# Narrow pooling bands, blocks of the first unit ended one by one, re-placed attention stages and a tail on four engines in a hybrid attention block

## The chip, the core and the metric

The kernel runs on one NeuronCore of a Trainium2 chip. The metric is the device time of one execution in microseconds. A kernel's time is the median of several executions; beside them one execution was profiled, and all rows of the profile come from that one. PE is TensorE, PEld its weight loads, DVE VectorE, ACT ScalarE, POOL GpSimd, SP the engine whose queue issues most DMAs.

## What is computed

One decoder layer for 1024 positions of width 1024, float32 throughout:

```python
h = rms_norm(x, ln_pre_mix)
proj = h @ w_in                       # 256 pooling channels, then q, k, v of 12 heads of 64
pool_out = multi_scale_pool(u_pool, w_pool, pool_scale)   # windows 2/4/8/16, 4 groups of 64 channels
attn_out = dilated_attention(rope(q), rope(k), v)          # windows (128,1), (512,4), (2048,16)
mix = concat(pool_out, attn_out) @ w_out
x = x + rms_norm(mix, ln_post_mix)
h = rms_norm(x, ln_pre_ffn)
f = (silu(h @ w_gate) * (h @ w_up)) @ w_down
x = x + rms_norm(f, ln_post_ffn)
```

In the pooling mixer each group's channels are averaged over a trailing window, the token itself is subtracted, and a 64x64 map and a per-channel scale follow.

## The kernel before

**Products.** Activations lie transposed, channels on the partitions. Each float32 operand is split into a high and a low part (`split`, `into`), ACT copying the high part and DVE or POOL subtracting for the low one; a product is then three matmuls (`PASSES`: high-high, high-low, low-high).

**Stages.** First the norm and the q/k projection of head pair 0. Then the "first unit" with `rows_first`, which projects the values of pairs 0 and 1 and the pooling channels together, in two halves of 512 positions; each half has four blocks of 128 positions, four weight tiles `i` and two contraction tiles `kk` in each, and one PSUM bank per block (`pj` for blocks 0 and 1, `t` for 2 and 3, two buffers each). When a block has its last product, ACT and DVE take it out as high and low parts, into the tile `vs` (one buffer, two blocks fill it, then one DMA stores it to `vd`) and into `u`. Then `pool_bands` and `pool_means` make the window means as products of `u` with a band matrix, 144 columns wide (a block and the 16 positions after it), and `pool_product` applies the 64x64 maps.

**Attention units.** Six head pairs times two halves are twelve units, numbered by `turn_of`. A unit has these stages: `scores` (8 steps; DVE masks and takes the maximum in one instruction, ACT exponentiates), `merge`/`join` (the weights `wv` from maxima and sums, small DVE steps around one pair of small matmuls `e`), `weigh` (16 scalings of score blocks by `wv`, on POOL or DVE), `turn` (PE transposes the weighted blocks, ACT and DVE split them into `ptr`) and `product` (values). `rope` of later pairs and the projections of later q, k and v run between them.

**What sets the order.** PE executes in program order. `put(steps, lo, hi)` places each stage's steps on a time axis whose unit is an attention unit; `emit` sorts all steps by place. The table `PRM` (`G`) holds the places: `h0`, `h1` for units of the first and second half, `first` and `last` for the end units, `du` for additions per unit, `pm` for the bands, `c0` to `c3` for norm chains and block sums after the attention. `Fill` lists hold projection matmuls; `await_` pulls further fill steps ahead of a stage while the planner's own clock is below the stage's due time, at most `fl` of them. On the other engines a scheduler orders the instructions, and `high_priority(offset)` ranks the small stages (score masks and exponentials, merges, the splits of `turn`) above their place; `hp` is that offset, doubled for a merge. `wd` says for each of the 16 scalings whether POOL (0) or DVE (1) takes it, `we` which `w_in` tiles are split by DVE (1) instead of POOL, `rk`, `rq`, `r0` to `r3` on which engine a rope's sine product and its sum run (0 POOL, 1 DVE).

**After attention.** `out_proj` in two halves, norms (`chain`), the gated feed-forward as seven block products per pair of tiles (`seven`), after six tiles' first products (`firsts`), then the down projection (`down`, products P1 to P3 in the order P1, P6, P2, P7, P4, P5, P3). The last product P3 is cut into columns 0 to 256 and 256 to 512, each ended by `End.finish`: `mean` (PE sums the squares of `sq` and of the last square `jk`), a POOL power, `rows` (PE transposes the factors into a PSUM row block `rb`), `times` (DVE multiplies four 128-row blocks at once) and `plus` (adds `x`, then stores).

Of the kernel before, what the change touches and what calls it, by code (L numbers as in the profile page):

```python
# [1765 lines left out]
```

## Time and profile before

| | |
|---|---|
| median of 3 runs | 1148.39 us |
| lowest, highest | 1147.02, 1149.25 us |
| profiled execution, its own time | 1147.94 us |
| its span, first to last instruction | 1146.2 us |
| PE busy | 1122.9 us (98%), 5916 matmuls |
| PE weight loads | 964.5 us (84%) |
| DVE, ACT, POOL busy | 825.2 (72%), 553.0 (48%), 548.6 us (48%) |
| DMA | 201.59 MB, 176 GB/s over the span |
| mean granted clock of PE | 0.989 |

Matmuls are pipelined, so PE's busy time says that something was in the array, not that it streamed at its peak; the ends of matmuls are modelled, and a few matmul records can be missing. A row of the timeline reads: start, length, engine, line, operation, output tile, inputs, shape, number of instructions merged, and in brackets how long the engine sat idle before it and which instruction ended that. A wait is put down to the semaphore that came last by the profile; where the engine named had long been done, it was another.

### The profile page before, as it was taken

Reading aid. Unit: us, or ns where it says so; the run is one execution under the profiler, and the core shown is the slowest. Engines: PE = TensorE matmul, PEld = TensorE weight load, DVE = VectorE, ACT = ScalarE, POOL = GpSimd, SP = SyncE. Lnnn points to the kernel's source line nnn. Section 1 sums busy time; section 2 is a strip of 40 time slices with the busy share of each in tenths; the row PEclk is TensorE's granted clock in tenths of the full one; section 3 lists DMA queues with packets and bytes.
Section 4 is the critical chain, followed back from the end, with each engine's and each line's share of the span. In section 5 each row is a group of like instructions: output and inputs, shape, how many; then the busy total and the mean of one; then the engine's idle time right before and its main releaser. Section 6 shows DMA issues by size and latency. Waiting matters only on the chain. (4 is left out here: it accounts for less than half of the span.)

```text
span 1146.2 us, 16886 instructions
## 1 busy us (share of the span) xinstructions
PE 1122.9 (98%) x5916; PEld 964.5 (84%) x5916; DVE 825.2 (72%) x1525; ACT 553.0 (48%) x1048; POOL 548.6 (48%) x488
## 2 busy tenths in 40 slices
PE   9999999999998999999999999999999999999996
PEld 7888998989888888888888888888888888888896
DVE  7956888887988684979867777675666477343684
ACT  7345766666666674767422222332233425343441
POOL 0030535364465222020067677875587859666520
PEclk9998999999998999999999999999999999999998
DMA  8215151515126655754566666433543879566442
GB/s 279 99 59 187 39 183 38 183 39 184 56 92 219 204 201 193 286 198 170 193 210 239 244 249 235 173 126 140 202 166 150 283 261 312 193 198 199 131 147 74
DMA packets 91140, 201.59 MB, mean 176 GB/s; under 512 B 9264, under 2 KB 25136, under 8 KB 89648
## 3 DMA queue, kind: packets, MB, share of 16 engines
q1 hardware_dynamic: 90080, 199.74, 50.0%
q8 instruction: 46, 0.75, 0.3%
q10 hardware_dynamic: 976, 0.79, 0.2%
q14 instruction: 38, 0.31, 0.1%
HBM read 143.61 MB, written 56.89 MB: 175 GB/s over the span
## 5 line engine op out<-in xcount | busy, mean ns | idle before, releaser
L167 PE MATMUL ps_o<-tT,fw 128*128 128x512 f32 x648 | 151.2, 390 | 0.0
L167 PEld LDWEIGHTS ps_o<-tT,fw 128*128 128x128 f32 x648 | 121.4, 188 | 26.2 <-issue 0.3
L167 PE MATMUL ps_pj<-x,whl 128*128 128x512 f32 x480 | 142.9, 411 | 0.0
L1249 POOL TENSOR_TENSOR fw<-rw,fw 128x512 fp32r<-128x512 f32 x74 | 103.2, 1418 | 29.5 <-ACT fw L1247 29.4
L702 POOL TENSOR_SCALAR pp<-pp,wv 128x256 f32<-128x256 f32 (+1 forms) x144 | 70.8, 511 | 71.3 <-DVE wv L682 71.3
L639 ACT ACTIVATE pp<-pp,sx 128x128 f32<-128x128 f32 (+1 forms) x192 | 89.2, 467 | 29.5 <-DVE sx L636 28.6
L213 POOL TENSOR_TENSOR whl<-wraw,whl 128x512 fp32r<-128x512 f32 x40 | 53.1, 1351 | 87.0 <-ACT whl L209 79.7
L167 PEld LDWEIGHTS ps_pj<-x,whl 128*128 128x128 f32 x480 | 85.8, 190 | 9.8
L1544 POOL TENSOR_TENSOR op<-rw,op 128x512 fp32r<-128x512 f32 x38 | 61.1, 1607 | 40.4 <-ACT op L1543 38.6
L239 POOL TENSOR_TENSOR nrr<-nrr,half 128x4 f32<-128x4 f32 (+1 forms) x7 | 7.4, 1060 | 142.7 <-ACT eps L238 99.4
L167 PE MATMUL ps_s<-b,fw 128*128 128x512 f32 x312 | 73.3, 392 | 0.0
L167 PE MATMUL ps_pj<-whl,x 128*128 128x256 f32 (+1 forms) x432 | 72.1, 305 | 0.3 <-POOL whl L213 0.3
L1545 DVE TENSOR_TENSOR op<-rw,op 128x512 fp32r<-128x512 f32 x33 | 45.2, 1369 | 34.4 <-ACT op L1543 34.3
L167 PEld LDWEIGHTS ps_s<-b,fw 128*128 128x128 f32 x312 | 58.6, 188 | 13.0
L1543 ACT ACTIVATE op<-rw 128x1024 fp32r<-128x1024 f32 x38 | 40.0, 1058 | 60.4 <-PE ps_t L167 30.3
L1249 POOL TENSOR_TENSOR whl<-rw,whl 128x512 fp32r<-128x512 f32 x30 | 47.4, 1602 | 42.2 <-ACT whl L1247 26.9
L1247 ACT ACTIVATE fw<-rw 128x1024 fp32r<-128x1024 f32 x45 | 47.5, 1061 | 40.5 <-PE ps_o L167 16.0
L747 ACT ACTIVATE ptr<-ps_t 128x512 fp32r<-128x512 f32 (+1 forms) x84 | 48.5, 577 | 37.0 <-PE ps_t L170 34.1
L748 DVE TENSOR_TENSOR ptr<-ps_t,ptr 128x512 fp32r<-128x512 f32 (+1 forms) x84 | 56.0, 667 | 13.7 <-ACT ptr L747 13.3
L167 PEld LDWEIGHTS ps_pj<-whl,x 128*128 128x128 f32 x432 | 60.1, 194 | 2.2 <-POOL whl L213 0.5
L167 PE MATMUL ps_o<-ptr,v 128*128 128x128 f32 (+1 forms) x472 | 57.4, 256 | 0.6 <-DVE ptr L748 0.6
L167 PEld LDWEIGHTS ps_o<-ptr,v 128*128 128x128 f32 x472 | 52.6, 164 | 3.9 <-DVE ptr L748 1.1
(312 smaller groups left out, 2862.6 us busy)
## 6 DMA issues: line engine op xcount, KB each, us to landing
rw<-bd SPq DMA_DIRECT2D x77, 256.0 KB, 4.1
rw<-in_w_gate_dram SPq DMA_DIRECT2D x28, 512.0 KB, 4.6
rw<-in_w_up_dram SPq DMA_DIRECT2D x28, 512.0 KB, 5.4
v<-vd SPq DMA_DIRECT2D x22, 512.0 KB, 3.9
rw<-wsd SPq DMA_DIRECT2D x44, 256.0 KB, 3.8
bd<-p SPq DMA_DIRECT2D x39, 256.0 KB, 2.2
rw<-in_w_down_dram SPq DMA_DIRECT2D x33, 256.0 KB, 3.9
wraw<-in_w_out_dram SPq DMA_DIRECT2D x15, 512.0 KB, 4.5
```

Source lines behind the costliest of these rows:

```text
L167: return tc.keep_in_program_order(nc.tensor.matmul(*a, **k))
L213: pin(eng.tensor_tensor(dst[:, 1, at:at + w], src[:, at:at + w], dst[:, 0, at:at + w].bitcast(F32), ALU.subtract))
L239: powers.append(nc.gpsimd.tensor_tensor(r, r, half.to_broadcast([P, n]), ALU.pow))
L639: nc.scalar.activation(pt[:, j, lo:], pt[:, j, lo:], AF.Exp, bias=sx[:, 0, side, j, hd, 0:1], scale=-1.0, accum_out=sx[:, 0, side, j, hd, ...
L702: nc.gpsimd.tensor_scalar(pv, pv, un.wv[:, side, j, hd:hd + 1], 1.0, op0=ALU.mult, op1=ALU.mult)
L747: nc.scalar.activation(ptr[:, 0, :w], t[:, :w], AF.Copy)
L748: nc.vector.tensor_tensor(ptr[:, 1, :w], t[:, :w], ptr[:, 0, :w].bitcast(F32), ALU.subtract)
L1247: nc.scalar.activation(dst[:, :, 0], src, AF.Copy)
L1249: low[0] = eng.tensor_tensor(dst[:, i, 1], src[:, i], dst[:, i, 0].bitcast(F32), ALU.subtract)
L1543: nc.scalar.activation(w[:, :, 0], raw, AF.Copy)
L1544: nc.gpsimd.tensor_tensor(w[:, 0, 1], raw[:, 0], w[:, 0, 0].bitcast(F32), ALU.subtract)
L1545: (nc.gpsimd if p == "P1" else nc.vector).tensor_tensor(w[:, 1, 1], raw[:, 1], w[:, 1, 0].bitcast(F32), ALU.subtract)
```

## The change

1. `pool_means` handles one group (`n`) per call. Its stationary operand is the group's own 64 columns of `u` instead of the 128 columns of two groups, and the result lies in partitions 0 to 63 of the bank. The two groups of a call before are placed apart (`pn` in the place of `pm`), and the pooling product has a place of its own.
2. `rows_first`: in the first half the last two weight tiles, and in the second half the last three, run block by block, instead of all blocks per weight tile.
3. `out_proj`, first half: the first two output blocks take four contraction tiles each, then three each, then the third block follows; the third block is in bank `s`, the first two in `pj`.
4. Ranks: `hk` gives chosen units' score, merge and turn stages an offset of their own; `hp` is 210 instead of 150.
5. Places: most numbers of `first`, `h0`, `h1`, `du`, `vt`, `pw`, `lr`, `lw0`, `lc`, `c0` to `c3`, `n0` to `n2` and the planner's `lm`, `lw`, `fl`. `cut` interleaves the end of one and the start of the next fill list in unit 7. `tv` emits turns and products of units 5, 8 and 11 together, `sg` stops fill between dilated scores in units 5, 10 and 11.
6. Engines: `wx` moves scalings of single units (2 is ACT), `rx` gives single ropes' engines as (half-pair key): (sine product, sum), `we` and `fe` move splits, `jp` keeps `nm` and `dd` of the merge in the PSUM bank of `e`.
7. `End.mean` emits the sums of `sq` first and those of the last square after them. The last cut's `times` and `plus` become `last`, in which DVE, POOL, ACT and PE share the four pairs of row blocks.

```diff
- 'we': (0, 0, 0, 0, 1, 1, 1, 0, 0, 0, 1, 1),
- 'nt0': 0.505,
+ 'we': (1, 1, 0, 0, 0, 0, 1, 0, 0, 1, 1, 1),
+ 'nt0': 0.53225,
- 'hp': 150,
- 'fl': 15,
+ 'hp': 210,
+ 'fl': 17,
- 'lm': 3.036,
- 'lw': (3.551, 0.5),
+ 'lm': 3.054,
+ 'lw': (3.821, 0.21),
- 'n1': 0.29735,
+ 'n1': 0.36647,
- 'first': {'s0': 0.4784, 's1': 0.61071, 'm': 0.68269, 'w0': 0.77241, 'w1': 1.06, 't0': 1.1},
+ 'first': {'s0': 0.52619, 's1': 0.59216, 'm': 0.6494, 'w0': 0.77955, 'w1': 1.04288, 't0': 1.1},
- 'cut': {},
+ 'cut': {7: (1, 6, 17)},
...
-        9: {'m': 0.0183, 'w1': -0.0101, 't1': -0.0102, 's1': -0.0286, 'v0': 0.0055, 'v1': 0.0156},
+        9: {'m': -0.0661, 'w1': 0.0469, 't1': -0.0086, 's1': -0.0326, 'v0': 0.0055, 'v1': -0.032,
+            's0': 0.0653, 'w0': -0.0375},
- 'pm': (0.9242, (0.75639, 0, 0), (0.85679, 1, 0), (1.01653, 0, 1), (1.05, 1, 1)),
+ 'pm': 0.92623,
+ 'pn': ((0.75947, 0.77947, 0.8194699999999999),
+        (0.85757, 0.8775700000000001, 0.91757),
+        (1.01653, 1.03653, 1.07653),
+        (1.0512, 1.0712, 1.1112))}
- 'fe': ((1, 1), (1, 1), (0, 1), (0, 1), (1, 1), (1, 1), 1),
- 'sg': (0, 0, 0, 0, 0, 0, 0, 0, 0, 0, 0, 0),
- 'wx': {},
- 'tv': (0, 0, 0, 0, 0, 0, 0, 0, 0, 0, 0, 0),
- 'jp': 0,
+ 'fe': ((1, 1), (1, 1), (1, 1), (0, 1), (1, 1), (1, 1), 1),
+ 'sg': (0, 0, 0, 0, 0, 1, 0, 0, 0, 0, 1, 1),
+ 'wx': {0: {9: 2, 12: 0}, 3: {7: 2, 4: 2}, 9: {5: 0, 2: 0, 0: 0},
+        6: {5: 2, 14: 2, 15: 0, 4: 2, 1: 1, 11: 2, 8: 0}, 5: {9: 0}, 8: {14: 2, 1: 0, 2: 2, 10: 2},
+        7: {15: 2, 10: 1, 2: 0, 1: 2}, 4: {12: 0, 7: 1, 11: 2, 2: 1, 5: 2, 1: 2}, 1: {10: 0, 11: 0, 12: 0},
+        11: {12: 1, 2: 0, 7: 1, 3: 2}, 10: {9: 2, 12: 0}, 2: {4: 0, 2: 1, 6: 2}},
+ 'tv': (0, 0, 0, 0, 0, 1, 0, 0, 1, 0, 0, 1),
+ 'jp': 1,
+ 'hk': {('s', 10): 0, ('j', 7): 450, ('t', 4): 150, ('t', 0): 300, ...
- 'rx': {},
+ 'rx': {(1, 3, 1): (0, 1), (1, 2, 0): (0, 0), (1, 1, 0): (0, 0), (0, 2, 0): (0, 0), (0, 2, 1): (0, 0),
+        (1, 5, 1): (1, 0), (0, 4, 1): (1, 0), (0, 1, 0): (0, 0), (0, 4, 0): (0, 0)},
...
+    def rank(what, pr, h):
+        return G["hk"].get((what, turn_of(pr, h)), G["hp"] * (2 if what == "j" else 1))
...
-        order += [(0, i, t) for i in (2, 3) for t in range(4)] + [(1, i, t) for i in (3, 2, 1, 0) for t in range(4)]
+        order += [(0, i, t) for t in range(4) for i in (2, 3)] + [(1, 3, t) for t in range(4)]
+        order += [(1, i, t) for t in range(4) for i in (2, 1, 0)]
...
-        sl = slice(i * P, (i + 1) * P)
-        for n in range(2):
-            g = 2 * i + n
-            ps = bank("o")
...
+        d, g, rows = pool.w["d", i, h], 2 * i + n, slice(64 * n, 64 * n + 64)
+        sl, ps = slice(64 * g, 64 * g + 64), bank("o")[0:64]
...
-                box[d] = box[d], bank("s" if d % 2 else "pj")
+                box[d] = box[d], bank("s" if d % 2 and (h or d > 2) or h == 0 and d == 2 else "pj")
...
+        if h == 0:
+            order = ([(d, k) for kk in (ks[:4], ks[4:7]) for d in range(2) for k in kk] + [(2, k) for k in ks[:7]]
+                     + [(d, 7) for d in range(3)])
...
                 for c in range(n):
-                    mm(sp[:, c:c + 1], self.sq[:, lo + c * P:lo + (c + 1) * P], ones, start=True, stop=False)
-                    mm(sp[:, c:c + 1], self.jk[lo][:, c * P:(c + 1) * P], ones, start=False, stop=True)
+                    mm(sp[:, c:c + 1], self.sq[:, lo + c * P:lo + (c + 1) * P], ones, start=(c == 0), stop=False,
+                       skip_group_check=True)
+                for c in range(n):
+                    mm(sp[:, c:c + 1], self.jk[lo][:, c * P:(c + 1) * P], ones, start=False, stop=(c == n - 1),
+                       skip_group_check=True)
...
+            def last():
+                rb = box["rb"]
+                row, pb = strip("q", 2)[:, :hi - lo], bank("s")
+                for c in range(n):
+                    turned_to(pb[:, c * P:(c + 1) * P], box["r"][:, c:c + 1].to_broadcast([P, P]), idt)
+                nc.scalar.activation(row, pb[:, :hi - lo], AF.Copy)
...
+                def times(a, to):
+                    pin(nc.vector.tensor_tensor(to, part[a][0], rb[:, None].to_broadcast([P, 2, hi - lo]), ALU.mult))
...
+                y, x = part[1, 0]
+                both = bank("pj")
+                mm(both, idt, x, start=True, stop=False)
+                times((1, 0), y)
+                y, x = part[1, 2]
+                nc.gpsimd.tensor_tensor(y, y, row[:, None].to_broadcast([P, 2, hi - lo]), ALU.mult)
+                y, x = part[1, 0]
+                mm(both, idt, y, start=False, stop=True)
+                nc.scalar.activation(y, wide(both), AF.Copy)
+                store(nc.scalar, (1, 0))
+                for a, tag in (((0, 0), "o"), ((0, 2), "t")):
+                    y, x = part[a]
+                    ps = wide(bank(tag))
+                    times(a, ps)
+                    w = 2 if tag == "o" else 1
+                    for k in range(0, 2, w):
+                        pin(nc.vector.tensor_tensor(y[:, k:k + w], ps[:, k:k + w], x[:, k:k + w], ALU.add))
+                        store(nc.sync, a, k, w)
+                y, x = part[1, 2]
+                nc.gpsimd.tensor_tensor(y, y, x, ALU.add)
+                store(nc.scalar, (1, 2))
```

More of the change, by code (lines that the diff above doesn't have):

```diff
@@ L634, in step @@
                     row, mask = (x.rearrange("p (r c) -> p r c", c=4) for x in (row, mask))
-                with tc.high_priority(offset=G["hp"]):
+                with tc.high_priority(offset=rank("s", pr, h)):
                     nc.vector.tensor_tensor_reduce(
@@ L644, in merge @@
     def merge(pr, h):
-        with tc.high_priority(offset=2 * G["hp"]):
+        with tc.high_priority(offset=rank("j", pr, h)):
             join(pr, h)
@@ L745, in turn @@
             ptr = turned[hd, gi] = att.tile([P, 2, 512], F32R, name="ptr", tag="ptr", bufs=PTB)
-            with tc.high_priority(offset=G["hp"]):
+            with tc.high_priority(offset=rank("t", pr, h)):
                 nc.scalar.activation(ptr[:, 0, :w], t[:, :w], AF.Copy)
@@ L869, in pool_means @@
         await_(("u", h))
-        d = pool.w["d", i, h] = att.tile([P, 2, 512], F32R, name="dhl", tag="ptr", bufs=PTB)
-        sl = slice(i * P, (i + 1) * P)
-        for n in range(2):
-            g = 2 * i + n
-            ps = bank("o")
-            bd = pool.a[:, 144 * g:144 * g + 144]
-            jobs = [(128 * t, 144 if t < 3 else 128, pool.u[h][b][:, t, sl], bd) for t in range(4) for b in range(2)]
-            if h:
-                jobs += [(0, 16, pool.u[0][b][:, 3, sl], bd[:, 128:]) for b in range(2)]
-            else:
-                jobs += [(0, 16, pool.u[0][b][:, 0, sl], pool.a[:, 576 + 64 * a + 16 * g:592 + 64 * a + 16 * g])
-                         for a, b in PASSES]
-            for m, (at, w, lhs, rhs) in enumerate(jobs):
-                mm(ps[:, at:at + w], lhs, rhs[:, :w], start=(m == 0), stop=(m == len(jobs) - 1), skip_group_check=True)
-            rows = slice(64 * n, 64 * n + 64)
-            nc.scalar.activation(d[rows, 0], ps[rows], AF.Copy)
-            nc.vector.tensor_tensor(d[rows, 1], ps[rows], d[rows, 0].bitcast(F32), ALU.subtract)
+        if n == 0:
+            pool.w["d", i, h] = att.tile([P, 2, 512], F32R, name="dhl", tag="ptr", bufs=PTB)
+        d, g, rows = pool.w["d", i, h], 2 * i + n, slice(64 * n, 64 * n + 64)
+        sl, ps = slice(64 * g, 64 * g + 64), bank("o")[0:64]
+        bd = pool.a[:, 144 * g:144 * g + 144]
+        jobs = [(128 * t, 144 if t < 3 else 128, pool.u[h][b][:, t, sl], bd) for t in range(4) for b in range(2)]
+        if h:
+            jobs += [(0, 16, pool.u[0][b][:, 3, sl], bd[:, 128:]) for b in range(2)]
+        else:
+            jobs += [(0, 16, pool.u[0][b][:, 0, sl], pool.a[:, 576 + 64 * a + 16 * g:592 + 64 * a + 16 * g])
+                     for a, b in PASSES]
+        for m, (at, w, lhs, rhs) in enumerate(jobs):
+            mm(ps[:, at:at + w], lhs, rhs[:, :w], start=(m == 0), stop=(m == len(jobs) - 1), skip_group_check=True)
+        nc.scalar.activation(d[rows, 0], ps, AF.Copy)
+        nc.vector.tensor_tensor(d[rows, 1], ps, d[rows, 0].bitcast(F32), ALU.subtract)
     def pool_product(i, h):
+        need(("means", i, h), 2)
         if i + h == 0:
@@ L1016, in hybrid_block @@
     put([pool_bands], G["pb"], 0)
-    put(Fill(rows_first()).by(3), 0.0, G["pm"][0])
-    for at, i, h in G["pm"][1:]:
-        put([lambda a=(i, h): pool_means(*a)], at, 0)
-        put([lambda a=(i, h): pool_product(*a)], at + 0.06, 0)
+    put(Fill(rows_first()).by(3), 0.0, G["pm"])
+    for at, (i, h) in zip(G["pn"], ((0, 0), (1, 0), (0, 1), (1, 1))):
+        for n in range(2):
+            put([lambda a=(i, h, n): pool_means(*a)], at[n], 0)
+        put([lambda a=(i, h): pool_product(*a)], at[2], 0)
     KS = ((2, 3), (4, 5), (6, 7), (0, 1))
@@ L1071, in out_proj @@
         ks = (2, 3, 4, 5, 0, 1, 6, 7)
-        order = ([(d, k) for kk in (ks[:7], ks[7:]) for d in range(parts) for k in kk]
-                 + [(d, k) for d in range(parts, NK) for k in ks])
+        order = [(d, k) for kk in (ks[:7], ks[7:]) for d in range(parts) for k in kk]
+        if h == 0:
+            order = ([(d, k) for kk in (ks[:4], ks[4:7]) for d in range(2) for k in kk] + [(2, k) for k in ks[:7]]
+                     + [(d, 7) for d in range(3)])
+        order += [(d, k) for d in range(parts, NK) for k in ks]
         return [lambda a=(d, k, k == ks[0], k == ks[-1], n): step(*a) for d, k in order for n in range(3)], weights
@@ L1614, in plus, with store, wide @@
                 queue.dma_start(out[at:at + 2 * P, 512 + lo:512 + hi].rearrange("(d p) t -> p d t", p=P), yd)
+            def last():
[4 more added lines that the diff above has]
+                nc.scalar.activation(row, pb[:, :hi - lo], AF.Copy)
+                part = {a: (yblock("%d2" % (a[0] + 1))[:, a[1]:a[1] + 2, lo:hi], self.x4[a[0]][:, a[1]:a[1] + 2, lo:hi])
+                        for a in ((1, 0), (1, 2), (0, 0), (0, 2))}
+                def store(queue, a, k=0, w=2):
+                    at = (4 * a[0] + a[1] + k) * P
+                    queue.dma_start(out[at:at + w * P, 512 + lo:512 + hi].rearrange("(d p) t -> p d t", p=P),
+                                    part[a][0][:, k:k + w])
+                def times(a, to):
+                    pin(nc.vector.tensor_tensor(to, part[a][0], rb[:, None].to_broadcast([P, 2, hi - lo]), ALU.mult))
+                def wide(ps):
+                    return ps.rearrange("p (d t) -> p d t", d=2)
+                y, x = part[1, 0]
[19 more added lines that the diff above has]
+                store(nc.scalar, (1, 2))
@@ L1616, in finish @@
+            if hi == 512 and self.h:
+                return [mean], [rows], [last]
             if not self.h:
                 return [mean], [rows], [lambda d=d: add(d) for d in range(NK)]
-            sums = ((1, 0, nc.gpsimd, nc.scalar, 1), (1, 2, nc.vector, nc.sync, 2), (0, 0, nc.vector, nc.scalar, 2),
-                    (0, 2, nc.vector, nc.sync, 2))
-            if hi < 512:
-                sums = [(n, i, nc.vector, nc.sync, 2) for n, i, *_ in sums]
+            sums = [(n, i, nc.vector, nc.sync, 2) for n in (1, 0) for i in (0, 2)]
```

42 lines of the change are left out of this document (21 added, 21 removed), and 206 rows, old and new, of the table PRM.

## The prediction

> **What bounds the kernel now.** I read the page first (span, busy shares), then the granted clock in stretches, then TensorE's own timeline at the places where the clock falls, then the other engines there, and last the chain that ends the run.
>
> ```profile
> span 1146.2 us, 16886 instructions
> PE 1122.9 (98%) x5916; PEld 964.5 (84%) x5916; DVE 825.2 (72%) x1525; ACT 553.0 (48%) x1048; POOL 548.6 (48%) x488
> ```
> ```profile
> 59.50:62.90 3.40, 3.40 (x12) 2.91 (x11) 2.96 (x10) 1.42 (x5) 0.00 (x0) 0.50 0.61 193
> 93.65:97.05 3.40, 2.85 (x25) 2.67 (x24) 2.30 (x8) 2.07 (x6) 0.00 (x0) 1.00 0.71 274
> 97.05:103.90 6.85, 6.85 (x29) 6.38 (x29) 2.07 (x3) 1.28 (x3) 0.00 (x0) 0.50 0.33 107
> 359.90:363.30 3.40, 1.04 (x9) 0.83 (x7) 3.26 (x5) 1.06 (x1) 3.40 (x4) 1.00 0.80 245
> 363.30:370.10 6.80, 5.98 (x28) 5.98 (x29) 6.65 (x15) 3.48 (x7) 6.80 (x13) 0.50 1.02 375
> 600.00:625.00 25.00, 25.00 (x111) 20.62 (x110) 18.82 (x23) 6.99 (x8) 19.63 (x14) 1.00 0.67 235
> ```
>
> TensorE is the bound: busy 98%, and in the feed-forward part (600 to 625) it runs 111 matmuls of 512 columns in 25 us, 225 ns each, with no gap. Nothing in the change touches that part, which fills everything from some 475 us to 1120 us. What can move lies in TensorE's work of the first 475 us, in its waits there, and in the tail. The rows above (columns: length, busy time and count of PE, PEld, DVE, ACT, POOL, then granted clock) show three stretches at half clock: 3.40, 6.85 and 6.80 us. Half clock loses half of each: 1.7, 3.4 and 3.4 us.
>
> **1. Pooling bands with 64 stationary columns.** 84 matmuls (x84 below) multiply 144, 128 or 16 columns with a 128-column stationary tile of which only 64 outputs are used.
>
> ```profile
> L167 PEld LDWEIGHTS ps_o<-ptr,v 128*128 128x128 f32 x236 | 43.3, 190 | 1.3
> L167 PEld LDWEIGHTS ps_o<-ptr,v 128*64 128x64 f32 x236 | 32.4, 137 | 2.6 <-DVE ptr L748 1.1
> L167 PEld LDWEIGHTS ps_o<-band,u 128*128 128x128 f32 x84 | 11.8, 221 | 0.9 <-DVE dhl L886 0.6
> 84.42 2.52 PE L167 MATMUL ps_o<-band,u 128*128 128x144 f32 x22
> 86.79 3.00 PE L167 MATMUL ps_t<-k,x 128*128 128x512 f32 x12
> 93.85 2.41 PE L167 MATMUL ps_o<-band,u 128*128 128x144 f32 x20
> 96.81 4.22 PE L167 MATMUL ps_o<-band,u 128*128 128x144 f32 x20 [0.55 <-DVE dhl L886]
> 100.89 1.20 PE L167 MATMUL ps_pj<-x,whl 128*128 128x512 f32 x2
> L885 ACT ACTIVATE dhl<-ps_o x6: 574/592/594, 85.7 to 101.1; 64x512 fp32r<-64x512 f32 x6
> L886 DVE TENSOR_TENSOR dhl<-ps_o,dhl x6: 682/689/695, 86.4 to 101.7; 64x512 fp32r<-64x512 f32 x6
> ```
>
> One run of 22 lasts from 84.42 to 86.79: 108 ns each. Streaming 144 columns would take 144/512 x 225 = 63 ns, so the load sets the pace. A 64-column load takes 137 instead of 190 ns. One end of the gain: 84 x 53 = 4.5 us. Other end: none, if evictions become the pace (rivals). Between them, at the streaming pace: 84 x (108 - 65) = 3.6 us. I take **3.8**, nearer to the rows of TensorE than to the evictions, because the groups are now emitted one by one, 0.02 of a unit apart, with projection matmuls between; copies per group stay the same.
>
> **2. The half clock behind the second half's bands.** In 93.65 to 97.05, PE waited at most 0.55 us, but the bands there stream only 63 of 108 ns or less; the half clock follows at once, and the next 20 bands need 4.08 us. With narrow loads the array streams nearly without pause. I take the 6.85 us stretch as gone: **3.4**, and the 0.55 wait: **0.5**. Ends: 0 and 3.9.
>
> **3. First unit's blocks end one by one.**
>
> ```profile
> 53.99 0.38 SPq L852 DMA_DIRECT2D vd<-vs  x1
> vd<-vs SPq DMA_DIRECT2D x12, 512.0 KB, 3.1
> 57.08 0.47 ACT L842 ACTIVATE vs<-ps_t,n1r 128x256 fp32r<-128x256 f32 x1 [2.98 <-DVE sx L636]
> 58.98 0.47 PE L167 MATMUL ps_t<-w,x 128*128 128x512 f32 x1 [1.59 <-DVE u L847]
> ```
>
> PE waits 1.59 us for the eviction of block 2. ScalarE starts that eviction only at 57.08, after 2.98 us idle; the named DVE step is a neighbour. The tile `vs` has one buffer, its store was issued at 53.99 and takes 3.1 us: 57.09. Now the order: of the last 48 matmuls of the first half, blocks 0 to 3 end after 30, 36, 42, 48; afterwards after 12, 24, 36, 48. Block 1, which lets the first store go, ends 12 x 225 ns = 2.7 us sooner, so the wait of 1.59 goes with 1.1 us to spare. Late next is the eviction of block 3, which still has 18 matmuls (4.1 us) before its bank is used. Behind the wait comes the 3.40 us stretch at half clock. I take 1.6 + 1.7 = **3.3**. Ends: 0 (the later place of the second `ropes`, 0.297 to 0.366, can put its DVE and ACT steps among these evictions) and 3.3.
>
> **4. Attention units: new places, ranks, engines.** The one large wait is in unit 9:
>
> ```profile
> 364.12 1.12 PE L170 MATMUL ps_t<-idt,pp 128*128 128x128 f32 x4 [3.19 <-POOL pp L702]
> 358.73 1.30 POOL L403 TENSOR_TENSOR rsw<-rsw,sinr 128x512 f32<-128x512 f32 x1 [7.84 <-DVE rsw L401]
> 359.98 2.52 POOL L213 TENSOR_TENSOR whl<-wraw,whl 128x512 fp32r<-128x512 f32 x2
> 362.44 1.28 POOL L406 TENSOR_TENSOR rco<-rco,rsw 128x512 f32<-128x512 f32 x1
> 358.48 0.67 DVE L402 TENSOR_TENSOR rco<-ps_pj,cosr 128x512 f32<-128x512 f32 x1
> 357.73 0.18 DVE L674 TENSOR_TENSOR dd<-nm,sx 128x32 f32<-128x32 f32 x1
> 359.67 0.41 DVE L677 TENSOR_TENSOR de<-dd,sx 128x32 f32<-128x32 f32 x1
> 360.11 1.19 DVE L678 TENSOR_TENSOR nm<-de 128x16 f32<-128x16 f32 x1
> 361.63 0.90 DVE L682 TENSOR_TENSOR wv<-nm,dd 128x16 f32<-128x16 f32 x1
> L167 PE MATMUL ps_s<-ex,ls x48: 217/275/323, 74.2 to 414.8; 128*128 128x64 f32 x48
> ```
>
> The weights `wv` are late because POOL is full and small DVE steps take 0.41, 1.19 and 0.90 instead of 0.18 us, each ending with a POOL instruction (360.03, 361.3, 362.5); the step that reads PSUM (L402) does not stretch. Three edits meet here. `jp` keeps `nm` and `dd` in PSUM: L677 and L682 get 0.23 + 0.72 = 0.95 us shorter; L678 still reads two SBUF tiles. `rx` gives the sine product of this very rope (pair 4, second half) to DVE: 1.30 us less on POOL ahead of the weights. `du` puts unit 9's merge 0.084 of a unit earlier, and a unit is (414.8 - 74.2)/11 = 31 us: 2.6 us, against an unmoved first turn. 2.6 + 1.3 alone exceeds 3.19. So 3.2 + 3.4 (its half clock) = **6.6**; ends 0 and 6.6. The Trainium skill (SBUF — State Buffer, "SBUF: two separate sides") calls the port pair of VectorE and GpSimd an exclusive lock, taken by a DVE instruction with two SBUF inputs; the trace agrees, 1.19 against 0.18 us, and without that rule 0.95 of the sum for `jp` would be 0, which the 3.9 us beside it cover.
>
> But all twelve units are re-placed: 18 of the 192 scalings go to ACT, others between POOL and DVE, ranks change, the fill of units 7 and 8 is interleaved, two splits move from DVE to POOL and one back. An ACT step of 256 columns costs 0.47 (L842 above) where ACT is half idle; the price of a bad place is a PE wait. Nothing before shows those waits, so I bound them: below, smaller waits go away, 2 us gained; above, one wait like unit 9's, 6.6. I set **two waits like the first unit's, +6.6 in all**, since that is the nearer size.
>
> **5. Output projections, norms, first feed-forward blocks.** In the first projection the matmuls stay; the third block alone holds an `s` bank now, and starts later, so scores have two banks longer. The norm chains and block sums get new places, and one operand split goes from POOL to DVE (`fe`).
>
> ```profile
> PE ps_o L170 <- POOL nrr L239: 0.5, 1, 0.5
> 525.00:550.00 25.00, 25.00 (x111) 20.52 (x110) 25.00 (x39) 15.58 (x24) 0.00 (x0) 1.00 0.33 115
> ```
>
> PE's one wait there is 0.5 us, for the rows of a norm; between 525 and 550 DVE has no idle time and POOL no work, but PE has no gap either. Ends: 0.5 gained, or 3.3 lost (a wait like the first unit's, if DVE falls behind). I take 0, since PE ran through DVE's fullest stretch.
>
> **6. The tail.**
>
> ```profile
> 1134.48 0.42 ACT L1568 ACTIVATE p<-y 128x256 f32<-128x256 f32 x1 [3.00 <-DVE y L1635]
> 1136.80 0.45 PE ps_pj L170 x2
> 1137.27 2.35 DVE y L1605 x2
> 1138.63 1.41 POOL L1610 TENSOR_TENSOR y<-y,xe 128x256 f32<-128x256 f32 x2 [1.88 <-issue]
> 1139.63 0.96 DVE y L1610
> 1141.19 0.60 DVE y L1610
> ```
>
> Now, from the transposes' end (T = 1137.25), DVE works alone until 1141.79. After: the two squares' products that need nothing run ahead, leaving two of four steps behind the last square, about 0.2. Then DVE has four steps of 512 columns and two of 256: 4 x 0.6 + 2 x 0.33 = 3.1. POOL: two more transposes 0.45, ACT copy 0.42, two passes of 1.41: T + 3.7 and handoffs. So the last store is issued some 3.85 after T instead of 4.54; with the 0.2: **0.95**. TensorE's identity sum is two full-precision products of 512 columns. No such width stands in the trace; `ex` products take two passes (x48 for 24), so 2 x 0.225 each, 0.9 at half clock; the second waits for DVE's first step and ends by T + 2.3, ACT's copy of 0.6 by T + 3, and even at twice the passes by T + 4.8. It is covered in the first case and the end in the last. Ends: 0.2 lost and 1.6 gained. By the lock rule above no DVE step here stretches, since each has one PSUM operand; without it, POOL's 2.8 us would be added to DVE's 3.1, and the tail would lose 1.4.
>
> **Sum** on the profiled execution, 1147.94: 3.8 + 3.9 + 3.3 + 6.6 + 0.95 = 18.6 gained, 1129.4; with +6.6, 1136.0. The median of the runs lies 0.45 above that execution: **1136.4**.
>
> **Rivals.** (a) Everything goes and no new wait comes: 1129.8. For: each has a mechanism above. Against: nearly every place in the attention part is moved.
> (b) Unit 9's wait stays, because weight splits (2.52) stay in POOL's queue: 1136.4 + 6.6 = 1143.
> (c) The bands don't get faster: two `o` banks, and a group's copy and subtraction take 0.59 + 0.69, as long as two groups' narrow matmuls would (2 x 0.65), so any handoff makes PE wait again (as 0.55 before): no 3.8, 1140.2; with the half clock too, 1144.1.
> (d) The half clock at 97 us is not of the bands. The Trainium skill (TensorE: Matmul & The Clock Gate, "HAM oscillation — how this bites in real kernels") lets the clock fall after an idle gap of more than about 3.4 us. This trace shows it falling with no gap over 0.55 us. If something other than the bands' low streaming makes it fall, the stretch stays: 1139.8.
> (e) Slower: ACT's in-order queue. A scaling given to ACT stands behind a step that waits, as L842 stood 2.98 us; the transposes of that unit wait, 3.2 plus half clock 3.4. Nine units hold such scalings. From 1129.8, four units with that wait give 1156; at fewer than four the kernel still gains.
>
> **Chances.** Forecast 0.48 (its own range 1132 to 1141), (a) 0.13, (b) 0.15, (c) 0.06, (d) 0.08, (e) 0.07, and 0.03 that gains and new waits cancel. About 0.2% (2.3 us) is what this kernel's measurement tells from no change. Faster: all of the forecast, (a), (d) and most of (b) and (c): 0.87; same 0.06; slower 0.07. Leaving out the lower half of (a), (e), and the upper part of (b): 1128.5 to 1145.
>
> **What would show it.** Bands of 128*64 in runs under 1.6 us for 22; clock 1.00 from 93 to 104 and from 57 to 63; PE without a wait over 1 us for `pp`; de and wv at 0.2 us; last store issued under 4 us after the first transposes. Wrong if a unit shows a new wait on `pp` or `ptr` with half clock behind it, or if PE waits for `dhl`.

## The result and the profile after

The changed kernel takes 1139.47 us (median; 1138.65 to 1141.23) where the kernel before, beside it, takes 1148.32 (1146.48 to 1150.83). The ratio is 0.9927, 95% interval 0.9912 to 0.9942: 0.7% faster. The forecast was 1136.4 us, with a range of 1128.5 to 1145.

The page of the kernel after opens so; the profiled execution took 1139.3 us.

```profile
span 1137.5 us, 16902 instructions
PE 1120.4 (98%) x5922; PEld 958.1 (84%) x5922; DVE 807.6 (71%) x1516; ACT 559.1 (49%) x1068; POOL 550.6 (48%) x481
```

To see where 8.7 us of span went, cut both spans at the same seven events: first band product, last band product, last value product, first and last product of `tT` (the feed-forward's inner part), first transposes of the tail, end. Before:

```profile
0.00:76.46 76.46, 71.61 (x323) 59.02 (x324) 59.62 (x121) 43.91 (x86) 6.44 (x11) 0.98 0.45 151
76.46:100.67 24.21, 23.42 (x138) 21.02 (x137) 12.42 (x30) 10.93 (x23) 7.46 (x14) 0.93 0.37 132
100.67:444.00 343.33, 337.00 (x2262) 309.65 (x2261) 281.54 (x810) 227.65 (x591) 149.84 (x196) 0.99 0.39 133
444.00:561.73 117.73, 117.22 (x532) 96.11 (x531) 97.47 (x146) 77.06 (x122) 12.04 (x10) 1.00 0.62 222
561.73:913.43 351.70, 351.70 (x1548) 289.27 (x1547) 239.25 (x267) 100.31 (x119) 246.24 (x177) 1.00 0.56 201
913.43:1136.80 223.37, 221.50 (x1120) 189.21 (x1118) 130.34 (x148) 93.13 (x107) 125.16 (x80) 1.00 0.59 194
1136.80:1146.20 9.40, 0.43 (x2) 0.19 (x2) 4.51 (x5) 0.00 (x0) 1.41 (x2) 0.57 0.34 112
```

After:

```profile
0.00:72.98 72.98, 70.45 (x327) 58.42 (x328) 59.68 (x119) 44.53 (x89) 5.19 (x10) 1.00 0.46 158
72.98:92.30 19.32, 18.42 (x144) 16.33 (x144) 11.83 (x31) 10.28 (x21) 9.92 (x16) 1.00 0.45 165
92.30:434.82 342.52, 337.29 (x2257) 308.44 (x2255) 278.88 (x800) 233.64 (x608) 148.83 (x190) 1.00 0.39 133
434.82:551.98 117.16, 117.16 (x529) 95.71 (x529) 98.80 (x148) 76.09 (x122) 9.95 (x7) 1.00 0.61 223
551.98:906.08 354.10, 353.17 (x1549) 289.02 (x1548) 239.01 (x267) 100.31 (x119) 245.21 (x177) 1.00 0.55 200
906.08:1129.28 223.20, 221.55 (x1121) 189.20 (x1119) 116.07 (x148) 93.30 (x107) 128.94 (x80) 1.00 0.59 194
1129.28:1137.50 8.22, 2.37 (x8) 1.01 (x8) 3.34 (x6) 0.98 (x2) 2.53 (x2) 0.84 0.39 128
```

The length stands behind the stretch; then come busy time and count of PE, PEld, DVE, ACT and POOL; PE's granted clock is the third column from the end. Up to the bands the kernel gained 3.5 us, in the bands 4.9, in the attention units 0.8, in the first products behind them 0.6, in the last part and the tail 0.2 and 1.2. The inner feed-forward, 351.70 before, takes 354.10: it **lost 2.4**, in a part where TensorE runs the same 1548 products in the same order.

The bands and unit 9 in TensorE's timeline of after:

```profile
72.98 1.54 PE L276 MATMUL ps_o<-band,u 128*64 128x144 f32 x22
74.38 0.94 PE L276 MATMUL ps_t<-whl,x 128*128 128x512 f32 x3
89.36 0.81 PE L276 MATMUL ps_o<-band,u 128*64 128x144 f32 x10 [0.90 <-DVE dhl L997]
94.41 0.97 PE L276 MATMUL ps_o<-dhl,wp 128*128 128x512 f32 x3 [0.70 <-DVE dhl L997]
353.20 1.20 PE L279 MATMUL ps_t<-idt,pp 128*128 128x128 f32 x4 [2.00 <-POOL pp L814]
```

Twenty-two band products now last 74.38 - 72.98 = 1.40 us, 64 ns each instead of 108: the pace of streaming. But PE now waits 0.90 and 0.70 us for the last operand splits of the bands, and unit 9's wait of 3.19 us is 2.00, not gone. (`dhl` is the pooling means in two parts, `pp` the weighted score blocks that the transposes take.) Of the three stretches at half clock inside the kernel one is left, half as long, behind unit 9's wait:

```profile
353.11:356.51 3.40, 3.31 (x16) 3.06 (x16) 3.28 (x7) 1.54 (x3) 3.40 (x7) 0.51 0.91 322
```

The tail:

```profile
1129.28 0.43 PE L279 MATMUL ps_pj<-idt,nrr 128*128 128x128 f32 x2 [1.03 <-POOL nrr L348]
1129.75 0.69 DVE L1750 TENSOR_TENSOR y<-y,ps_pj 128x512 f32<-128x512 f32 x1 [1.30 <-PE ps_pj L279]
1129.77 1.02 PE L276 MATMUL ps_pj<-xe,idt 128*128 128x512 f32 x2
1130.43 1.26 POOL L1759 TENSOR_TENSOR y<-y,q 128x512 f32<-128x512 f32 x1 [1.20 <-ACT q L1740]
1130.63 1.02 PE L276 MATMUL ps_pj<-y,idt 128*128 128x512 f32 x2
1131.08 0.69 DVE L1770 TENSOR_TENSOR y<-ps_o,xe 128x512 f32<-128x512 f32 x1
1131.83 1.91 SPq L1746 DMA_DIRECT2D out_dram<-y  x3
1132.40 0.76 DVE L1770 TENSOR_TENSOR y<-ps_t,xe 128x256 f32<-128x256 f32 x2
```

DVE ends at 1133.16, 3.88 us after the start of the transposes; before it took 1141.79 - 1136.80 = 4.99 us. Each product of the identity sum takes two passes, as assumed, but a pass takes 0.43 us at full clock (the second product starts 0.86 us after the first), not 0.225. DVE's steps of 512 columns keep 0.69 us while POOL works beside them (1130.43 to 1131.69 against the one at 1129.75). The Trainium skill (SBUF — State Buffer, "SBUF: two separate sides") says that a DVE step takes the port pair that it shares with GpSimd when it is in a two-port mode or has two SBUF inputs; these steps each have one PSUM input, and the trace agrees.

### The profile page after: what moved, and what is told of

Same layout as the page of the kernel before. It is cut to its first block, busy times and chain, and to the rows that moved or that the text cites. A ratio compares the mean times of both kernels' runs of the same rounds, so it can differ in the third digit from the quotient of the medians.

```text
span 1137.5 us, 16902 instructions
## 1 busy us (share of the span) xinstructions
PE 1120.4 (98%) x5922; PEld 958.1 (84%) x5922; DVE 807.6 (71%) x1516; ACT 559.1 (49%) x1068; POOL 550.6 (48%) x481
## 4 chain that ended last, share of the span: by engine, by line
PE 87%; DVE 6%; POOL 3%; DMA 2%; issue 1%; ACT 1%; SPq 0%; ACTq 0%; DVEq 0%; POOLq 0%
PE ps_pj L276 28%; PE ps_s L276 25%; PE ps_o L276 22%; PE ps_t L276 10%; PE ps_t L279 3%; DMA rw<-in_w_up_dram 1%; POOL fw L1365 1%; POOL pp L814 1%; DVE pp L748 1%; DVE ptr L860 1%; DVE rsw L510 0%; POOL whl L1464 0%; DMA wraw<-in_w_in_dram 0%; ACT pp L751 0%; DVE ql L542 0%
## 5 line engine op out<-in xcount | busy, mean ns | idle before, releaser
L276 PE MATMUL ps_pj<-x,whl 128*128 128x512 f32 x480 | 138.1, 407 | 0.3 <-DVE whl L322 0.3
L814 POOL TENSOR_SCALAR pp<-pp,wv 128x256 f32<-128x256 f32 (+1 forms) x135 | 67.8, 523 | 111.5 <-DVE wv L794 111.5
L1365 POOL TENSOR_TENSOR fw<-rw,fw 128x512 fp32r<-128x512 f32 x72 | 100.3, 1416 | 30.2 <-ACT fw L1363 30.1
L751 ACT ACTIVATE pp<-pp,sx 128x128 f32<-128x128 f32 (+1 forms) x192 | 89.3, 468 | 31.5 <-DVE sx L748 30.9
L276 PE MATMUL ps_pj<-whl,x 128*128 128x256 f32 (+1 forms) x432 | 68.4, 299 | 0.0
L1661 DVE TENSOR_TENSOR op<-rw,op 128x512 fp32r<-128x512 f32 x33 | 28.8, 872 | 40.1 <-ACT op L1659 29.9
L276 PE MATMUL ps_s<-k,qh 128*128 128x128 f32 (+1 forms) x192 | 54.4, 295 | 1.9 <-DVE sx L748 1.5
```

The lines of the kernel that those rows point to most:

```text
L276: return tc.keep_in_program_order(nc.tensor.matmul(*a, **k))
L751: nc.scalar.activation(pt[:, j, lo:], pt[:, j, lo:], AF.Exp, bias=sx[:, 0, side, j, hd, 0:1], scale=-1.0, accum_out=sx[:, 0, side, j, hd, ...
L814: nc.gpsimd.tensor_scalar(pv, pv, un.wv[:, side, j, hd:hd + 1], 1.0, op0=ALU.mult, op1=ALU.mult)
L1365: low[0] = eng.tensor_tensor(dst[:, i, 1], src[:, i], dst[:, i, 0].bitcast(F32), ALU.subtract)
L1661: (nc.gpsimd if p == "P1" else nc.vector).tensor_tensor(w[:, 1, 1], raw[:, 1], w[:, 1, 0].bitcast(F32), ALU.subtract)
```

## The experiments

Ratios are to the kernel before, timed on the same chip in the same series. The first eight stood beside a before of 1146.25 or 1146.82 us, the last four beside 1147.06.

### Are the narrow bands or the block order the cause of the early gain?

`e1_wide` puts the 128-column stationary tile back and leaves the order, the places and everything else.

```diff
-        sl, ps = slice(64 * g, 64 * g + 64), bank("o")[0:64]
+        sl, ps = slice(i * P, i * P + P), bank("o")
...
-        nc.scalar.activation(d[rows, 0], ps, AF.Copy)
+        nc.scalar.activation(d[rows, 0], ps[rows], AF.Copy)
```

> The changed kernel with the pooling bands' stationary operand back at 128 columns (all else as changed). If narrow loads save what the rows say: 84 matmuls go from about 64 to 108 ns, 3.7 us more, and if the bands' low streaming is what halves the clock, a half-clock stretch of 3.4 or 6.8 us comes back near 90 us: 1139.5 + 3.7 = 1143.2, with half clock 1145 to 1147. Rival (the evictions are the pace, PE waits for dhl anyway): the waits for dhl of 0.9 and 0.7 us vanish as the bands get longer, and the kernel loses only about 2: 1141.5, clock 1.00.

Measured: 1143.74 us, ratio 0.9973 (0.9962 to 0.9983). Its last band product comes 3.50 us later than in after (95.80 against 92.30), and nothing is won back up to unit 9's merge (also 3.5). Behind that PE waits 1.63 us for a DMA at 379; `e3_shift128`, which has narrow bands, shows such a wait of 1.46 us there, so it is not of the bands. In its timeline and its stretches:

```profile
89.23 2.29 PE L276 MATMUL ps_o<-band,u 128*128 128x144 f32 x20
92.02 1.28 PE L276 MATMUL ps_o<-band,u 128*128 128x144 f32 x10 [0.49 <-DVE dhl L997]
```
```profile
90.40:93.82 3.42, 2.93 (x24) 2.80 (x24) 1.38 (x2) 1.86 (x5) 0.00 (x0) 1.00 0.76 289
```

So the narrow load is worth some 3.5 us (3.4 counted from the first band product). But in this profile the clock did not fall, here or anywhere else before the tail, although the bands are wide again: the forecast of a half-clock stretch near 90 us missed, and wide loads alone need not bring one. That is one execution; what another may do is taken up in the section on the prediction.

`e2_order` keeps the narrow bands and puts the blocks of the first unit back as they were.

```diff
-        order += [(0, i, t) for t in range(4) for i in (2, 3)] + [(1, 3, t) for t in range(4)]
-        order += [(1, i, t) for t in range(4) for i in (2, 1, 0)]
+        order += [(0, i, t) for i in (2, 3) for t in range(4)] + [(1, i, t) for i in (3, 2, 1, 0) for t in range(4)]
```

> The changed kernel with the old order of the first unit's blocks (all blocks per weight tile). If the single vs tile and its store set the wait: blocks 0 and 1 end 2.7 us later, PE waits 1 to 2 us near 55 us and a half-clock stretch of 3.4 us follows: 1139.5 + 3 = 1142.5. Rival (the wait went away because the second half's ropes were moved, not because of the order): no wait over 0.5 us there, 1139.5.

Measured: 1147.49 us, ratio 1.0009 (0.9994 to 1.0023): no gain is left. Its timeline and the stretch behind the bands:

```profile
58.23 1.18 PE L276 MATMUL ps_t<-w,x 128*128 128x512 f32 x4 [1.97 <-DVE u L959]
90.61 0.28 PE L276 MATMUL ps_o<-band,u 128*64 128x144 f32 x1 [0.91 <-ACT u L955]
91.52 0.34 PE L276 MATMUL ps_o<-band,u 128*64 128x144 f32 x2 [0.63 <-DVE u L959]
94.05 0.81 PE L276 MATMUL ps_o<-band,u 128*64 128x144 f32 x10 [0.76 <-DVE dhl L996]
```
```profile
94.91:98.31 3.40, 3.40 (x15) 2.92 (x15) 1.06 (x4) 0.57 (x1) 0.00 (x0) 0.50 0.02 5
```

The first unit's wait is back (1.97 us), this time with no half clock behind it. In the second half the bands must now wait for `u`: the four blocks end six products apart instead of eighteen, and ACT and DVE take them out one after the other. Half clock follows. The last band product comes 6.22 us later than in after. The forecast for this run, 1142.5, was 5 us too fast. The block order is the largest single part, and by time its second half, which the prediction gave no price, is the larger share of it: 2.15 us had come by the first band, 4.1 came after it. (The run puts back both halves at once; the split is read from its timeline.)

### Where did the feed-forward lose 2.4 us?

The pitch of the matmuls (start to start) answers. In the same stretch of before, after and of three kernels described below, a run of 24 products of `b` and the row behind it, whose start ends the 24 pitches; before:

```profile
584.93 5.67 PE L167 MATMUL ps_s<-b,fw 128*128 128x512 f32 x24
590.44 5.65 PE L167 MATMUL ps_o<-tT,fw 128*128 128x512 f32 x24
```

after:

```profile
575.18 5.76 PE L276 MATMUL ps_s<-b,fw 128*128 128x512 f32 x24
580.78 5.62 PE L276 MATMUL ps_o<-tT,fw 128*128 128x512 f32 x24
```

5.51 us became 5.60, that is 229.6 and 233.3 ns each. By groups over the whole trace, 792 products with `b` moving went from 229.3 to 233.3 ns (3.2 us in all), products of `tT` and `fw` stayed at 227, and the 24 with `fw` moving and `b` stationary went the other way, 233.4 to 229.0. What moved is an address: `nm` and `dd` are in PSUM now (`jp`), the pool ahead is 128 B smaller, and `b` lies at 160 instead of 32 modulo 256 B in its partition. The weights and `tT` lie at 224. (These are the places that the built programs give their tiles; a profile does not show them.) An unused tile ahead of the feed-forward's tiles tests that.

```diff
     ffnl = ctx.enter_context(tc.tile_pool(name="ffnl", bufs=1))
+    ffnl.tile([P, BYTES // 4], F32, name="shift")
```

`BYTES` is 128 in `e3_shift128` and `e10_before_plus128`, 64 in `e4_shift64` and `e12_shift64_again`, 192 in `e9_before_plus192` and `e11_old_places_plus192`.

> The changed kernel with an unused tile of 128 bytes per partition ahead of the feed-forward tiles, which puts them at the addresses of the kernel before. Theory A (in the feed-forward part, products whose moving operand is a block b stream 233.3 ns apart instead of 229.3 because jp made the pool of small tiles 128 bytes smaller and so moved these blocks against the stationary tiles): b products at 229.3 again, some 820 x 4 = 3.3 us less, 1136.2. Rival B (the slower spacing comes from what the other engines do at that time): 233.3 stays, 1139.5.

Measured: 1138.82 us, ratio 0.9932 (0.9911 to 0.9953). The products of `b` are back at 229.3 ns and `b` stands at 32, but the forecast time of 1136.2 missed: the ratio can't be told from that of the changed kernel. In the profile the stretch from the first product of `b` to the tail is 1.9 us shorter than in after (644.5 against 646.3), not 3.2, and ahead of it 2.6 us are lost, 1.46 of them in a wait for a DMA at 378.

> As the last, but 64 bytes: moving blocks and stationary tiles then have the same address modulo 256 bytes, as the pairs that run at 226.7 ns have. Theory A with a period of 256 bytes: b products at 226.7, some 820 x 6.6 = 5.4 us less, 1134.1. With a period of 2048 bytes only: somewhere between, 229 to 233. Rival B: 233.3 and 1139.5.

Measured: 1135.69 us, ratio 0.9905 (0.9886 to 0.9924). The timeline of this kernel:

```profile
574.83 5.60 PE L276 MATMUL ps_s<-b,fw 128*128 128x512 f32 x24
580.27 5.60 PE L276 MATMUL ps_o<-tT,fw 128*128 128x512 f32 x24
```

5.44 us for 24: 226.7 ns each, the figure of the `tT` products. `b` and the weights are both at 224. From the first product of `b` to the tail it takes 641.2 us, 5.2 less than after, which is 792 x 6.6 ns.

The same was then done to the kernel before, with nothing of the change in it.

> The kernel before, with an unused tile of 192 B ahead of the feed-forward's tiles, so that its moving blocks b lie at 224 modulo 256 B in a partition, like the stationary tiles, instead of at 32. Theory of the two addresses: the products fw,b go from 229.3 to 226.7 ns for 512 columns (some 820 of them, 2.1 us), so 1144.7 where the kernel before has 1146.8, ratio 0.998, and all places before 480 us as before. Rival (the pitch hangs on the tile's own address, or the tile's move only matters in the changed kernel): 229 ns stays or another figure comes, ratio 1.000.

Measured: 1144.58 us, ratio 0.9983 (0.9970 to 0.9995); 5.44 us for 24, 226.7 ns:

```profile
583.33 5.60 PE L167 MATMUL ps_s<-b,fw 128*128 128x512 f32 x24
588.77 5.60 PE L167 MATMUL ps_o<-tT,fw 128*128 128x512 f32 x24
```

> The kernel before, with an unused tile of 128 B ahead of the feed-forward's tiles, so that its blocks b lie at 160 modulo 256 B, as they do in the changed kernel. Theory of the two addresses: the products fw,b go from 229.3 to 233.3 ns (some 820, 3.3 us), those the other way round from 233.4 to 229; 1149 to 1150 where the kernel before has 1146.8, ratio 1.002 to 1.003: the loss that the changed kernel took in its feed-forward, without anything else of the change. Rival (the loss there came from the new places of norms and splits): 1146.8, ratio 1.000.

Measured: 1149.69 us, ratio 1.0023 (1.0009 to 1.0036). Its timeline:

```profile
585.17 5.76 PE L167 MATMUL ps_s<-b,fw 128*128 128x512 f32 x24
590.77 5.62 PE L167 MATMUL ps_o<-tT,fw 128*128 128x512 f32 x24
```

The pitch of the changed kernel, 5.60 us for 24, arises in the kernel before from the address alone. The rival, that new places of norms and splits cost it, is out for the pitch.

### What are the new places worth, and what `jp`?

`e5_old_places` is the changed code with the table of before (`PRM`): old places, ranks and engines, `jp` 0, the two groups of a call 0.02 apart.

```diff
- 'hp': 210,
+ 'hp': 150,
- 'jp': 1,
- 'hk': {('s', 10): 0, ('j', 7): 450, ...
+ 'jp': 0,
+ 'hk': {},
...
```

> The changed kernel's code (narrow bands placed one by one, new block order, new projection order, new tail) with the table of the kernel before: old places, ranks, engines, jp 0. jp 0 also puts the feed-forward tiles back at the addresses of before, 3.4 us faster in that part. Theory (the attention part's new places gain little: 0.8 us net between the last band and the last value product): first-unit part about as in the changed kernel (8 us ahead of before), unit 9's wait of 3.2 us with its 6.8 us at half clock back, 1139.5 - 3.4 + 4 = 1140. Rival (the places carry the gain): the lead at the last band falls to about 4, and the kernel stands at 1144 to 1146.

Measured: 1140.28 us, ratio 0.9945 (0.9923 to 0.9967). The merges of units 3 to 7 come 9.9 us earlier than in before, about as early as in after, so bands and block order bring that with any table. In unit 9 the old wait and the old half clock are there:

```profile
354.62 1.11 PE L171 MATMUL ps_t<-idt,pp 128*128 128x128 f32 x4 [3.18 <-POOL pp L706]
```
```profile
353.49:360.31 6.82, 5.69 (x27) 5.70 (x28) 6.67 (x15) 3.19 (x6) 6.82 (x13) 0.50 1.03 396
```

`e6_jp0` puts back only `nm` and `dd` into SBUF.

```diff
- 'jp': 1,
+ 'jp': 0,
```

> The changed kernel with jp 0 alone: nm and dd of the merges in SBUF again. Theory (jp gives nearly nothing, since its merge steps sum to 14.7 us against 15.1 before, and it costs 3.4 us by moving the feed-forward tiles): b products at 229.3 ns, 1139.5 - 3.4 = 1136. Rival (the merge steps behind POOL set unit 9's first turn): L678 and L682 stretch to about 1 us, unit 9's wait grows from 2.0 to about 3 us with another half-clock stretch of 1.7: 1138.5.

Measured: 1140.04 us, ratio 0.9946 (0.9925 to 0.9967), no difference from after. The forecast of 1136 missed. The products of `b` return to 229.3 ns, but by the last value product this profile is 2.4 us behind, 1.9 of them since unit 8's merge; unit 9's wait grows only from 2.00 to 2.19 us, and its half clock stays at 3.41. `jp` gave in attention about what it took in the feed-forward.

> The changed code with the old table of places (as in the run with old places, which took 0.9945 of before) and the unused tile of 192 B, so that b lies at 224. The sum of what was measured apart: 1140.3 less 2.1 us for the products fw,b, 1138.1, ratio 0.9925; unit 9's wait of 3.35 us with 6.8 us of half clock stays. If the new table of places is worth nothing once the addresses are equal, it would come out like the changed kernel shifted by 64 B, 1135.7, ratio 0.9905; theory: it stays 2 to 2.5 us behind that.

Measured: 1136.65 us, ratio 0.9912 (0.9892 to 0.9931). The last run has the new table at equal addresses, beside it.

> The changed kernel with the unused tile of 64 B once more, beside the three others and in five rounds: 0.9905 of before, some 2 us less than the changed kernel (0.9927), and 2 to 2.5 us less than the old places shifted by 192 B. The rival, that the first figure was a lucky one, says 0.9925 and no difference from the old places.

Measured: 1134.30 us, ratio 0.9891 (0.9872 to 0.9910). With equal addresses, 2.35 us lie between the old table and the new: that is what all new places, ranks and engines in attention and norms, `jp` with them, are worth. The intervals of the two ratios overlap; the two marks at the start of the feed-forward, 485.16 and 483.51 us, stand 1.65 us apart in the same direction. This version beats both kernels.

### The tail, and unit 9

`e7_old_tail` puts the old last cut back (`times` and `plus` on DVE and POOL) and keeps the new order in `mean`.

```diff
-            if hi == 512 and self.h:
-                return [mean], [rows], [last]
-            sums = [(n, i, nc.vector, nc.sync, 2) for n in (1, 0) for i in (0, 2)]
+            sums = ((1, 0, nc.gpsimd, nc.scalar, 1), (1, 2, nc.vector, nc.sync, 2), ...
```

> The changed kernel with the old times and plus at the end (mean keeps its new order). From the first transposes to the end of the span: 9.35 us before, 8.24 in the changed kernel. Theory: 9.3 again, 1.1 us more, 1140.6. Rival (the end is set by the stores' landing and the closing semaphores, whichever engine adds): less than 0.3 us more.

Measured: 1139.89 us, ratio 0.9948 (0.9930 to 0.9966). From the first transposes to the end it takes 9.12 us, after 8.24, before 9.35. The difference of 0.9 is rough: in this profile the transposes ran at half clock (0.69 us against 0.43), and from DVE's last step to the end it took 3.9 us instead of the 4.4 of before and after. DVE's own steps last 4.52 us here as before, 3.41 after, so the four engines bring 1.1. The medians differ by 0.4 us, the ratios by 0.002 with overlapping intervals: the times can't tell.

`e8_shift64_u9` is `e4_shift64` with the sine product of the rope that stands ahead of unit 9's merge (pair 5, second half of the queries) on DVE.

```diff
-        (1, 5, 1): (1, 0), (0, 4, 1): (1, 0), (0, 1, 0): (0, 0), (0, 4, 0): (0, 0)}
+        (1, 5, 1): (1, 0), (0, 4, 1): (1, 0), (0, 1, 0): (0, 0), (0, 4, 0): (0, 0), (0, 5, 1): (1, 0)}
```

> The changed kernel with the 64 byte shift and the sine product of the rope in unit 9 (pair 5, second half, queries) on DVE instead of POOL. Theory (POOL's queue ahead of the first scaling sets unit 9's wait): L512 of 1.28 us leaves POOL there, the 2.0 us wait for pp falls to about 0.8, its window streams over 0.40 and keeps the clock: 2.9 us less than with the shift alone, ratio to before 0.988. Rival (DVE, which makes wv, becomes late instead): the wait stays within 0.5 us of 2.0.

Measured: 1140.88 us, ratio 0.9947 (0.9928 to 0.9966), 5 us worse than `e4_shift64`. PE and DVE at that place:

```profile
358.73 1.20 PE L280 MATMUL ps_t<-idt,pp 128*128 128x128 f32 x4 [7.15 <-POOL pp L815]
352.81 2.93 DVE L542 CAST qh<-rco 64x512 fp32r<-64x512 f32 x2
355.77 1.41 DVE L543 TENSOR_TENSOR ql<-rco,qh 64x512 fp32r<-64x512 f32 x2
357.94 0.17 DVE L795 TENSOR_TENSOR wv<-total,ps_s 128x16 f32<-128x16 f32 x1
```

The rope ended sooner, so its casts became ready before the merge's last four small steps, and DVE took them first: 4.3 us. (ACT, too, had two casts of this rope in its queue ahead of the merge's exponential, which ran only at 353.8.) `wv` ended at 358.1 instead of 352.6, PE waited 7.15 us, and 10.2 us of half clock followed.

## Why the prediction was right, and where it was not

**Step 1, bands: right.** 3.8 taken, 3.5 measured by `e1_wide`; 64 ns for 108. Rival (c) came true in small: PE waits 1.6 us for the splits of `dhl`, 0.55 before.

**Step 2, half clock at 97 us: gone as forecast, but the cause named was only part of it.** The prediction held the wide loads to be the cause. The profile of `e1_wide` has wide loads and full clock, that of `e2_order` narrow loads and half clock. What counts in both is how much of a window TensorE streams, with waits and loads together (last section). By that count the full clock of `e1_wide` is in part luck: its window there began at 90.49 us and streamed 0.45; one that began between 89.3 and 90.1 would have streamed less than 0.40, which is where all falls lie. In after no window laid over the bands streams less than 0.55. So, by that count, wide loads let the clock fall in some executions, and narrow loads with the new block order in none. The time of rival (d) is out, since the stretch does not stay; its premise, that something beside the bands' own streaming makes the clock fall, `e2_order` bears out.

**Step 3, block order: right, and too low.** 3.3 taken, up to the first band 3.5 measured (2.15 in `e2_order`). The difference is the half clock behind the wait, which not every execution has: `e10_before_plus128`, the same program as before up to here, waits 1.61 us at this place and goes on at full clock, and so does `e2_order`.

```profile
58.86 0.47 PE L167 MATMUL ps_t<-w,x 128*128 128x512 f32 x1 [1.61 <-DVE u L847]
```
```profile
58.86:62.27 3.41, 3.41 (x18) 3.01 (x19) 3.12 (x11) 1.95 (x8) 0.00 (x0) 1.00 0.61 192
```

So the 1.7 that this step holds for half clock is earned only in a part of the executions. The second half's order was in the change and had no term; it is the larger share.

Steps 1 to 3 together were to bring 11.0; the merges of units 3 to 7 in `e5_old_places` show 9.9. The 1.1 that lack are near the new `dhl` waits less the old one (1.6 - 0.55); no run separates them.

**Step 4, attention: the term that failed for unit 9.** The prediction took `rx` to relieve POOL of the rope ahead of unit 9's merge. That rope is of pair 5's queries; `rx` has that pair's keys in this half, not its queries, and the sine product still takes 1.28 us on POOL. From the merge to POOL's first scaling it is 6.6 us, 8.6 before. But the first turn was not unmoved: PE reaches it 5.1 us after the merge, 5.8 before. So 1.2 us of wait and 1.7 of half clock went, 2.9 of the 6.6 forecast; rival (b) was half right. (The half clock is no accident of one execution: with the old places four of five profiles have two windows of it there and one has one, with the new ones seven have one and `e1_wide` has none.) `e8_shift64_u9` shows that the edit that the prediction believed in would have made it worse. The allowance of 6.6 for new waits did not arise in attention: PE waits 1.5 us in three places for `sx`, which is new, but no longer 1.9 for `ex`. Net of gain and allowance, step 4 was 0 in the forecast and is worth some 2.35 us with addresses equal, norms included. Of the `jp` term the trace shows that the steps with an input in PSUM no longer stretch, and that two merge steps with two SBUF inputs still do (L783, up to 1.15 us, and L790, up to 0.61); in unit 9:

```profile
348.69 0.90 DVE L783 TENSOR_TENSOR ps_s<-sx 128x16 f32<-128x16 f32 x1
351.27 0.17 DVE L789 TENSOR_TENSOR de<-ps_s,sx 128x32 f32<-128x32 f32 x1
351.48 0.61 DVE L790 TENSOR_TENSOR ps_s<-de 128x16 f32<-128x16 f32 x1
```

In the same step the count of splits is off: `we` moves two from DVE to POOL and three, not one, the other way.

**The feed-forward: the step that was missing.** "Nothing in the change touches that part" was wrong. `jp` moved the moving operand by 128 B: +3.2 us. PE also waits 0.9 us for `sq` at 679; a wait for `sq` in this part comes without the change, too (0.7 in `e9_before_plus192`, none in before).

**Step 5, output projections: right.** 0 taken; the stretch from the last value product to the first product of `tT` became 0.6 us shorter.

**Step 6, tail: right, a little low.** 0.2 was taken for the mean and 0.21 measured (`ACT p` to transposes 2.32, now 2.11); 0.75 for the rest (4.54 - 3.85, its own figures, give 0.69) and 1.1 measured by the profile, 0.9 by `e7_old_tail`. The identity sum, priced at 0.225 us a pass, took 0.43 and stayed covered. The last store is issued at 1133.34, 3.63 us after the end of the first transposes; 3.85 was worked out.

**The sum.** 1129.4 without any allowance, + 3.7 that unit 9 kept, + 3.2 of addresses, + 1.1 in the bands, + 0.9 for `sq`, - 0.4 of the tail gives 1137.9; the profiled execution took 1139.3. The remaining 1.4 lies in small pieces over attention that no run separates. The forecast of 1136.4 came near because an allowance of 6.6 us, put in for waits that did not come, had about the size of a shortfall and an address effect that it did not know: as a sum, that is luck.

Among the rivals, (e) says that with fewer than four such waits the kernel still gains; by its own figures three give 1129.8 + 19.8 = 1149.6, no gain. The kernel after shows no new wait of that size.

## What to carry to other kernels

After any edit that changes the size of a tile, compare the pitch of matmuls in the parts that you did not edit; where moving and stationary operands lie at different offsets, a few unused bytes can be worth as much as a rescheduling (here 792 x 6.6 ns = 5.2 us, against 2.35 for all re-placing). When blocks share evictions, let them end one by one rather than together. And a step moved to relieve one engine can make another step ready sooner and put it ahead of the one you wanted: look at who is next in the other engine's queue.
